# Retention block on one core: q and k of three heads by a seven-product scheme over halves of the tokens

## The chip, the cores and the metric

The kernel runs on one core of one Trainium2 chip. A core has a matrix engine (PE, with weight loads listed as PEld), a vector engine (DVE), a scalar engine (ACT), a general engine (POOL) and a queue engine (SP), which here only issues transfers. The metric is the device time of one execution in microseconds (us), as the median of several runs; lower is better.

## The reference

One encoder layer over 512 tokens of width 1024, in float32. A normalised input is multiplied by one wide matrix `w_in`, whose columns hold a short gated convolution, the queries and keys of four heads (256 columns each per head), values and gates (512 each per head) and two branch gates. What matters here is the part of q and k:

```python
h = rmsnorm(x, g_mix[l])
proj = h @ w_in[l]
...
qf = rotary(q.reshape(b, s, RET_HEADS, RET_QK_DIM)) * (RET_QK_DIM ** -0.5)
kf = rotary(k.reshape(b, s, RET_HEADS, RET_QK_DIM))

def rotary(t):            # cos, sin: position times frequency
    t1, t2 = t[..., : d // 2], t[..., d // 2:]
    return jnp.concatenate([t1 * cos - t2 * sin, t1 * sin + t2 * cos], axis=-1)
```

Behind it stand the retention itself (scores, decay, product with v, norm and gate), the merge with the convolution branch, an output projection, a gated feed-forward part and a last norm.

## The kernel before

All large products are made in three matmuls: both operands are split into a high part (rounded to the format fp32r) and a low rest, and high times high, high times low and low times high are summed in PSUM. The split of a weight tile of 128 x 1024 is a cast on ACT (line 167, tile `whi`) and a subtraction on DVE (line 168, tile `wlo`); there are five pairs of these tiles.

The weights come in the order of one list, `PLAN` (lines 56 to 116). An entry "c" is a block of 128 x 2048 numbers, used as it is; an entry "q" is one of seven forms (`FORMS`, line 51) of a matrix cut into two by two blocks: b11, t1, t2, b21, t3, t4, b22. The forms t1 to t4 are sums of blocks, which DVE makes in place in the raw tile (line 240) before the split. With them a product of 2 x 2 blocks takes seven products of blocks instead of eight; the sums on the side of the activations are made once (`sums`, line 594). `take` hands out the next weights and keeps at least two units made ahead (`AHEAD`).

The input stage runs head by head (line 636): for the heads behind the first a quad of the forms gives v and gate (`do_quad`, `strassen`, token-major, matmuls of 512 columns, line 365), and `do_qk` gives q and k. `do_qk` calls `feature_major` twice, for q and for k: a block of weights with 256 columns, two PSUM banks of 128 features x 512 tokens, 24 matmuls of 512 tokens into each (lines 280 to 282). The rotation takes the first bank as t1 and the second as t2 and is made by DVE in operations of 128 x 512: two products and one sum or difference for each half of the features (lines 616 to 618). The result is split into `hi` and `lo` (`keep`, line 556) and POOL stores both in DRAM.

`fm_quad` (line 324) is the form that the convolution's projections use later: seven products of 24 matmuls over 256 tokens (`prod`, line 321), with the result of a product being two feature blocks side by side in a bank, and combinations of the banks by ACT copies (`snap`, line 372) and DVE.

Small tiles of 128 x 512 (`t512`) come from one pool of nine, PSUM has eight banks. A scheduler sets the order of the instructions on each engine from the written program and its dependencies; so the splits and sums of later weights stand between the rotations of earlier ones, and the decay tables (`decays`, line 524, written behind the quads) are made in the first two v and gate quads. An engine carries out its own instructions in that order.

Of the kernel before, what the change touches and what calls it, by code (L numbers as in the profile page):

```python
# [12 lines left out]
F32 = mybir.dt.float32  # L13
F32R = mybir.dt.float32r
AF = mybir.ActivationFunctionType
ALU = mybir.AluOpType

P = 128
# [5 lines left out]
QK = 256  # L24
# [5 lines left out]
C_XC, C_GB, C_GC, C_Q, C_K, C_V, C_G, C_GA, C_GR = (  # L30
    0, 1024, 2048, 3072, 4096, 5120, 7168, 9216, 10240)
# [19 lines left out]
FORMS = ("b11", "t1", "t2", "b21", "t3", "t4", "b22")  # L51
# [4 lines left out]
def plan():  # L56

    out = []

    def a(name, col):
        out.append(("c", name, 0, 8, col, 256))

    def b(name, row, nk, col, nc):
        out.append(("c", name, row, nk, col, nc))

    def quad(c0, c1):
        for name in FORMS:
            for u in (0, 2):
                out.append(("q", ("w", c0, c1), name, u, 2))

    for c in (C_V, C_G):
        for r in (0, 512):
            b("w_in", r, 4, c, 512)
    for h in range(HEADS):
        if h:  # L80
            quad(C_V + h * VD, C_G + h * VD)
        a("w_in", C_Q + h * QK)
        a("w_in", C_K + h * QK)
    for c in (0, 512):
        quad(C_GA + c, C_GR + c)
    for c0, c1 in ((C_XC, C_GC), (C_XC + 256, C_GC + 256), (C_GB, C_GB + 256)):
        for name in FORMS:
            out.append(("q", ("x", c0, c1), name, 0, 4))
    for s in (2, 3):
        for c in (C_XC, C_GC, C_GB):  # L90
            a("w_in", c + s * 256)
    for h in range(HEADS):
        for c in (0, 512):
            b("w_r_out", h * VD, 4, c, 512)
    for name in FORMS:
        for u in (0, 2):
            out.append(("q", ("a",), name, u, 2))
    for r in (0, 512):
        for c in (0, 512):
            b("w_o", r, 4, c, 512)  # L100
    def f(q, *names):
        for n in names:
            out.append(("q", ("f", q), n, 0, 4))

    f(0, "b11", "b21", "b12", "b22")
    f(1, "b11", "b21")
    for q0, n in FF_PARTS:
        for q in range(max(q0, 1), q0 + n):
            f(q, *(x for x in FORMS[1:5] if q > 1 or x != "b21"))
            if q + 1 < NQ:  # L110
                f(q + 1, "b11")
            f(q, "t4", "b22")
        for name in FORMS:
            for u in range(0, n, 2):
                out.append(("q", ("d", q0), name, u, min(2, n - u)))
    return out


PLAN = plan()
BLOCKS = [x for x in PLAN if x[0] == "c"]  # L120

# [17 lines left out]
def block_kernel(ctx: ExitStack, tc: tile.TileContext, xT, xtok, wpack, wquad, cols, decs, rot, g_ffn, g_final, out):  # L139
    nc = tc.nc  # L140
# [11 lines left out]
    def misctile(n, name):  # L152
        return misc.tile([P, D + 8], F32, tag="misc", name=name)[:, 0:n]
# [4 lines left out]
    def t512(dt=F32):  # L158
        return tmp.tile([P, 512], dt, tag="t512", name="t512")

    def bank():
        return psum.tile([P, 512], F32, tag="bank", name="bank")

    def split(src, hi, lo, scale=None):

        if scale is None:
            nc.scalar.copy(hi, src)  # L167
            nc.vector.tensor_tensor(out=lo, in0=src, in1=hi.bitcast(F32), op=ALU.subtract)  # L168
        else:
            nc.scalar.activation(hi, src, AF.Copy, scale=scale)  # L170
            nc.vector.scalar_tensor_tensor(
                out=lo, in0=src, scalar=scale, in1=hi.bitcast(F32),
                op0=ALU.mult, op1=ALU.subtract)
# [85 lines left out]
    def take():  # L259
        if not ready:  # L260
            prefetch()
        x, units = ready.pop(0)
        while sum(len(u) for _, u in ready) < AHEAD and prefetch():
            pass
        return x, units
# [22 lines left out]
    def feature_major(rhs, evict, block0=0):  # L288

        c = Chunk()  # L290
        for m in range(2):
            ps = bank()
            for k in range(8):
                mm3(ps, c.w(k, m * P, P), act_pair(rhs, k), k == 0, k == 7)
            evict(block0 + m, ps)
# [17 lines left out]
    def prod(w, x, ps, start, stop=True):  # L313

        (wh, wl), (xh, xl) = w, x
        for s in range(2):
            o = ps[:, s * 256:(s + 1) * 256]
            for k in range(4):
                c = slice(k * 256 + s * P, k * 256 + (s + 1) * P)
                for i, (l, r) in enumerate(((wh, xh), (wh, xl), (wl, xh))):  # L320
                    nc.tensor.matmul(o, l[:, c], r[:, k], start=start and s == 0 and k == 0 and i == 0,  # L321
                                     stop=stop and k == 3 and i == 2, skip_group_check=True)

    def fm_quad(forms, ev11, ev21, ev22, ev12):

        def w():
            return take()[1][0]
        a, d, b = bank(), bank(), bank()
        prod(w(), forms["a11"], a, True)
        p1 = snap(a)  # L330
        prod(w(), forms["s1"], d, True)
        prod(w(), forms["s2"], a, False)
        u2 = snap(a)
        prod(w(), forms["a12"], b, True)
        nc.vector.tensor_tensor(out=p1, in0=b, in1=p1, op=ALU.add)
        ev11(p1)
        prod(w(), forms["s3"], a, False)
        u3 = snap(a)
        nc.vector.tensor_tensor(out=u3, in0=d, in1=u3, op=ALU.subtract)
        ev22(u3)  # L340
        prod(w(), forms["a22"], a, False)
        ev21(a)
        prod(w(), forms["s4"], d, False)
        nc.vector.tensor_tensor(out=u2, in0=d, in1=u2, op=ALU.subtract)
        ev12(u2)
# [24 lines left out]
    def snap(ps):  # L370
        t = t512()
        nc.scalar.copy(t, ps)  # L372
        return t
# [27 lines left out]
    def of(pair, o=0):  # L401
        return lambda k, sl: tuple(t[:, k, sl.start + o:sl.stop + o] for t in pair)
# [36 lines left out]
    rcs = misctile(D, "rcs").rearrange("p (i n) -> p i n", i=2)  # L439
# [102 lines left out]
    def kept(name):  # L542
        return dram.tile([P, 4, 512], F32, name=name)

    tabs = [dram.tile([P, 896], F32, name=f"tab{h}") for h in range(HEADS)]
    qkd = [(kept(f"qh{h}"), kept(f"ql{h}")) for h in range(HEADS)]
# [9 lines left out]
    def keep(dst, src):  # L556
        hi, lo = t512(F32R), t512(F32R)
        split(src, hi, lo)
        for d, t in zip(dst, (hi, lo)):
            store(d, t.bitcast(F32))  # L560

    def store(dst, t):
        nc.gpsimd.dma_start(dst, t)
# [6 lines left out]
    for dst, func in ((vd[0], AF.Copy), (sgd[0], AF.Silu)):  # L570
        def ev(nb, ps):
            t = t512()
            nc.scalar.activation(t, ps, func, scale=rtok[0][:, nb:nb + 1])
            store(dst[:, nb, :], t)
# [19 lines left out]
    def sums(a11, a12, a21, a22):  # L594
        out = {}
        for name, o, in0, in1, op in (
                ("s1", a22, a21, a22, ALU.subtract), ("s3", a21, a11, a21, ALU.subtract),
                ("s2", a11, a22, a11, ALU.subtract), ("s4", a12, a12, a11, ALU.add)):
            nc.vector.tensor_tensor(out=o, in0=in0, in1=in1, op=op)
            out[name] = form_tile()  # L600
            split(o, *out[name])
        return out

    xf = sums(*(xs[i][:, :, o:o + 256] for o in (0, 256) for i in range(2)))
    for n, i, o in (("a11", 0, 0), ("a12", 1, 0), ("a22", 1, 256)):
        xf[n] = tuple(t[i][:, :, o:o + 256] for t in xg)
    xforms = {n: of(t) for n, t in xf.items()}

    def do_qk(h):
        for j in range(2):  # L610
            pss = []
            feature_major(xg, lambda m, ps: pss.append(ps))
            cos, sin = rcs[:, 0, :], rcs[:, 1, :]
            for i, (c1, c2, op) in enumerate(((cos, sin, ALU.subtract), (sin, cos, ALU.add))):
                a, b = t512(), t512()
                nc.vector.tensor_tensor(out=a, in0=pss[0], in1=c1, op=ALU.mult)
                nc.vector.tensor_tensor(out=b, in0=pss[1], in1=c2, op=ALU.mult)
                nc.vector.tensor_tensor(out=a, in0=a, in1=b, op=op)
                keep([t[:, 2 * j + i, :] for t in qkd[h]], a)
# [16 lines left out]
    for h in range(HEADS):  # L636
        if h:
            do_quad(vd[h], sgd[h], AF.Silu)
        do_qk(h)
    for j in range(2):  # L640
        do_quad(gad[j], grd[j], AF.Sigmoid, AF.Sigmoid)
    decays()
# [50 lines left out]
    T1, T2 = slice(0, 256), slice(256, 512)  # L693
# [104 lines left out]
    p = do_scores(nxt[0], nxt[1])  # L798
# [3 lines left out]
    for h in range(HEADS):  # L802
# [3 lines left out]
        t = sg  # L806
        if h < HEADS - 1:
            p = do_scores(nxt[0], nxt[1])
# [15 lines left out]
    for names, hl in zip((("a11", "a12"), ("s1", "s3"), ("s2", "s4"), ("a22",)), zd):  # L824
        t = [big.tile([P, 2, 4, 256], F32R, tag="big", name="zform") for _ in hl]
# [279 lines left out]
    a, d, b = ([bank(), bank()] for _ in range(3))  # L1105
# [93 lines left out]
```

## Time and profile before

| What | us |
|---|---|
| median of 3 runs (range) | 1051.09 (1050.66 to 1052.85) |
| the profiled execution | 1050.25 |
| its span, first to last instruction | 1048.5 |
| PE busy | 1030.8 |
| DVE busy | 877.8 |
| ACT busy | 520.2 |
| one v and gate quad, 168 matmuls of 512 columns | 38.08 |
| one q and k block, 96 matmuls of 512 tokens | 21.76 |
| one `fm_quad` of the convolution, 168 matmuls of 256 tokens | 20.38 and 20.40 |

Busy times overlap, since the engines run beside each other. The chain of the page goes back from the last instruction to what released it at each step; it tells which engine's work sets the end. The first q and k block lies from 55.5 to 77.4 us, the others at 115.48, 175.32 and 235.16 us, each behind the v and gate quad of its head.

### The profile page before, as it was taken

The page shows a single profiled execution, that of the slowest core. Times are in us where ns is not written, and L with a number is a line of the kernel's source. Part 1 is how long each engine was busy: PE and PEld are TensorE (multiplying, and loading weights), DVE is VectorE, ACT ScalarE, POOL GpSimd, SP SyncE. Part 2 cuts the span into 40 slices and gives each one's busy share as a digit, 9 for nine tenths or more (in the row PEclk, how much of TensorE's full clock was granted, in tenths as well). Part 3 has the DMA queues.
Part 4 walks back from the last instruction along what each step waited for, and adds up shares of the span by engine and source line. Part 5 has one row for each costly group of instructions (what it writes and reads, how often), then busy time and mean ns, then how long its engine had stood idle before and what let it go on. Part 6 is the DMA issues. An engine that isn't in the chain of part 4 may idle for free.

```text
span 1048.5 us, 14888 instructions
## 1 busy us (share of the span) xinstructions
PE 1030.8 (98%) x5664; PEld 897.9 (86%) x5664; DVE 877.8 (84%) x1131; ACT 520.2 (50%) x697; POOL 126.3 (12%) x202
## 2 busy tenths in 40 slices
PE   8999999999999999999999989999999999999996
PEld 7788888888888998888878868889998999899985
DVE  6999786958777888698988987659998999889995
ACT  7546654453656445242532424445555565556553
POOL 0111111111101003202122320000002000110010
PEclk9999999999999999999999999999999999999999
DMA  9636647282645577819647897731319422663322
GB/s 323 233 107 213 218 159 244 91 272 89 217 135 192 183 256 245 315 32 355 239 134 188 198 341 266 241 107 36 91 36 274 124 83 79 187 155 101 121 38 84
DMA packets 52920, 183.46 MB, mean 175 GB/s; under 512 B 6896, under 2 KB 6896, under 8 KB 49264
## 3 DMA queue, kind: packets, MB, share of 16 engines
q1 hardware_dynamic: 36592, 131.12, 36.9%
q0 software_dynamic: 16256, 51.39, 16.4%
q8 instruction: 44, 0.72, 0.3%
q14 instruction: 28, 0.23, 0.1%
HBM read 137.66 MB, written 44.83 MB: 174 GB/s over the span
## 4 chain that ended last, share of the span: by engine, by line
PE 87%; DVE 4%; DMA 3%; issue 2%; ACT 2%; POOL 1%; SPq 0%; POOLq 0%; ACTq 0%; DVEq 0%
PE bank L365 31%; PE bank L321 27%; PE bank L280 10%; PE bank L282 9%; PE bank L281 9%; DMA yr<-t 2%; DMA zform<-z 1%; DMA big<-xT 1%; DVE t L769 1%; DVE wlo L168 1%; DVE bnst L764 0%; ACT whi L167 0%; POOL bnmv L767 0%; DVE big L1099 0%; DVE big L771 0%
## 5 line engine op out<-in xcount | busy, mean ns | idle before, releaser
L167 ACT CAST whi<-raw 128x1024 fp32r<-128x1024 f32 (+1 forms) x281 | 289.0, 1032 | 288.1 <-PE bank L365 74.0
L168 DVE TENSOR_TENSOR wlo<-raw,whi 128x1024 fp32r<-128x1024 f32 (+1 forms) x281 | 335.7, 1202 | 108.5 <-ACT whi L167 107.5
L321 PE MATMUL bank<-xform,whi 128*128 128x256 f32 x1440 | 260.3, 283 | 0.0
L321 PEld LDWEIGHTS bank<-xform,whi 128*128 128x128 f32 x1440 | 224.8, 192 | 0.7 <-ACT t L372 0.6
L321 PE MATMUL bank<-xform,wlo 128*128 128x256 f32 x720 | 203.7, 283 | 0.0
L365 PE MATMUL bank<-whi,big 128*128 128x512 f32 x548 | 172.7, 390 | 0.4 <-DVE big L1117 0.4
L240 DVE TENSOR_TENSOR raw<-raw 128x1024 f32<-128x1024 f32 (+1 forms) x124 | 148.4, 1205 | 1.7 <-DMA raw<-wquad 0.4
L321 PEld LDWEIGHTS bank<-xform,wlo 128*128 128x128 f32 x720 | 138.2, 192 | 0.0
L365 PEld LDWEIGHTS bank<-whi,big 128*128 128x128 f32 x548 | 102.7, 188 | 23.3 <-issue 0.8
L365 PE MATMUL bank<-wlo,big 128*128 128x512 f32 x274 | 106.7, 390 | 0.0
L365 PE MATMUL bank<-whi,xform 128*128 128x512 f32 x320 | 101.0, 389 | 0.0
L280 PE MATMUL bank<-whi,big 128*128 128x512 f32 x240 | 94.6, 396 | 2.6 <-ACT big L170 2.0
L281 PE MATMUL bank<-wlo,big 128*128 128x512 f32 x240 | 94.2, 393 | 0.0
L282 PE MATMUL bank<-whi,big 128*128 128x512 f32 x240 | 93.5, 393 | 0.1
L372 ACT COPY t<-bank 128x512 f32<-128x512 f32 x120 | 68.6, 586 | 37.8 <-PE bank L365 17.2
L280 PE MATMUL bank<-big,whi 128*128 128x512 f32 x224 | 87.1, 389 | 0.0
L281 PE MATMUL bank<-big,whi 128*128 128x512 f32 x224 | 87.1, 389 | 0.0
L282 PE MATMUL bank<-big,wlo 128*128 128x512 f32 x224 | 87.1, 389 | 0.0
L365 PEld LDWEIGHTS bank<-whi,xform 128*128 128x128 f32 x320 | 60.1, 188 | 12.5
L167 ACT CAST big<-t 128x512 fp32r<-128x512 f32 (+1 forms) x60 | 34.7, 580 | 61.8 <-DVE t L743 43.1
L365 PE MATMUL bank<-wlo,xform 128*128 128x512 f32 x160 | 62.2, 389 | 0.0
L365 PEld LDWEIGHTS bank<-wlo,big 128*128 128x128 f32 x274 | 51.4, 188 | 10.4
(175 smaller groups left out, 1416.2 us busy)
## 6 DMA issues: line engine op xcount, KB each, us to landing
raw<-wquad SPq DMA_DIRECT2D x124, 512.0 KB, 4.4
raw<-wpack SPq DMA_DIRECT2D x58, 512.0 KB, 5.2
z<-t POOLq DMA_DIRECT2D x24, 256.0 KB, 5.4
yr<-t POOLq DMA_DIRECT2D x24, 256.0 KB, 7.8
zform<-z POOLq DMA_DIRECT2D x6, 1024.0 KB, 13.0
v<-t POOLq DMA_DIRECT2D x16, 256.0 KB, 4.8
sg<-t POOLq DMA_DIRECT2D x16, 256.0 KB, 3.2
qh<-t POOLq DMA_DIRECT2D x16, 256.0 KB, 2.6
```

The source lines that it names most:

```text
L167: nc.scalar.copy(hi, src)
L168: nc.vector.tensor_tensor(out=lo, in0=src, in1=hi.bitcast(F32), op=ALU.subtract)
L240: nc.vector.tensor_tensor(out=t, in0=t, in1=raws[quad, more, u][:, 0:n], op=ALU.add)
L280: nc.tensor.matmul(ps, lh, rh, start=first, stop=False)
L281: nc.tensor.matmul(ps, lh, rl, start=False, stop=False)
L282: nc.tensor.matmul(ps, ll, rh, start=False, stop=last)
L321: nc.tensor.matmul(o, l[:, c], r[:, k], start=start and s == 0 and k == 0 and i == 0, stop=stop and k == 3 and i == 2, skip_group_check=True)
L365: nc.tensor.matmul(pss[tt], l, r[:, c], start=start and k == 0 and i == 0, stop=stop and k == n - 1 and i == 2, skip_group_check=True)
L372: nc.scalar.copy(t, ps)
L769: nc.vector.tensor_scalar(out=t, in0=ps, scalar1=mv[:, 0:1], scalar2=mv[:, 3:4], op0=ALU.subtract, op1=ALU.mult)
```

## The change

For the second to fourth head, q and k are one 2 x 2 problem: the two blocks of columns are q and k of the head (256 features each), and the tokens are cut into halves of 256. `fm_quad` makes it in seven products. Each of its four results is one of q or k for one half of the tokens, with the two halves of its features side by side in a tile of 128 x 512; the rotation multiplies both at once by the cosine and by the sine, each read twice, then makes a difference and a sum of 128 x 256. The split and the stores follow per result, with pieces of 256 tokens. The first head stays as it was.

```diff
@@ plan
     for h in range(HEADS):
         if h:
             quad(C_V + h * VD, C_G + h * VD)
-        a("w_in", C_Q + h * QK)
-        a("w_in", C_K + h * QK)
+            for name in FORMS:
+                out.append(("q", ("x", C_Q + h * QK, C_K + h * QK), name, 0, 4))
+        else:
+            a("w_in", C_Q)
+            a("w_in", C_K)
...
+    def qk_quad(h):
+
+        def ev(j, t):
+            def turned(ps):
+                ps = ps.rearrange("p (m t) -> p m t", m=2)
+                a, b = (t512().rearrange("p (m t) -> p m t", m=2) for _ in range(2))
+                for o, i in ((a, 0), (b, 1)):
+                    nc.vector.tensor_tensor(out=o, in0=ps, in1=rcs[:, i:i + 1, t].broadcast_to([P, 2, 256]),
+                                            op=ALU.mult)
+                nc.vector.tensor_tensor(out=a[:, 0], in0=a[:, 0], in1=b[:, 1], op=ALU.subtract)
+                nc.vector.tensor_tensor(out=a[:, 1], in0=a[:, 1], in1=b[:, 0], op=ALU.add)
+                hl = [t512(F32R).rearrange("p (m t) -> p m t", m=2) for _ in range(2)]
+                split(a, *hl)
+                for d, x in zip(qkd[h], hl):
+                    store(d[:, 2 * j:2 * j + 2, t], x.bitcast(F32))
+            return turned
+        T1, T2 = slice(0, 256), slice(256, 512)
+        fm_quad(xf, ev(0, T1), ev(0, T2), ev(1, T2), ev(1, T1))
...
     for h in range(HEADS):
         if h:
             do_quad(vd[h], sgd[h], AF.Silu)
-        do_qk(h)
+            qk_quad(h)
+        else:
+            do_qk(h)
```

Lines of the changed kernel are three higher from `fm_quad` on (168 becomes 171, 240 becomes 243, 321 becomes 324) and 22 to 24 higher behind `do_qk`. The order on the engines changes with it. The places below are those at which PE and DVE, or PE and ACT, meet.

On DVE in the third head (the second of the changed ones), before: the rotation of q with the weight sums (`raw`) and splits (`wlo`) of the next quad between its steps.

```order
L616 TENSOR_TENSOR t512_1564<-bank_1514,rcs_142 128x512
L168 TENSOR_TENSOR wlo_1595<-raw_1432,whi_1594 128x1024
L240 TENSOR_TENSOR raw_1432<-raw_1432,raw_1500 128x1024
L617 TENSOR_TENSOR t512_1565<-bank_1539,rcs_142 128x512
L168 TENSOR_TENSOR wlo_1680<-raw_1414,whi_1679 128x1024
L618 TENSOR_TENSOR t512_1564<-t512_1564,t512_1565 128x512
L240 TENSOR_TENSOR raw_1414<-raw_1414,raw_1586 128x1024
L168 TENSOR_TENSOR t512_1570<-t512_1564,t512_1569 128x512
```

The same place in the changed kernel, from the split of the quad's first weights (`wlo_1788`) on, the first twelve of the 31 operations up to the split of its b21; L338 is the sum of `fm_quad` that gives the first result.

```order
L171 TENSOR_TENSOR wlo_1788<-raw_1633,whi_1787 128x1024
L243 TENSOR_TENSOR raw_1633<-raw_1633,raw_1696 128x1024
L338 TENSOR_TENSOR t512_1631<-bank_1601,t512_1631 128x512
L171 TENSOR_TENSOR wlo_1830<-raw_1663,whi_1829 128x1024
L619 TENSOR_TENSOR t512_1728<-t512_1631,rcs_142 128x512
L619 TENSOR_TENSOR t512_1729<-t512_1631,rcs_142 128x512
L243 TENSOR_TENSOR raw_1663<-raw_1663,raw_1740 128x1024
L621 TENSOR_TENSOR t512_1728<-t512_1728,t512_1729 128x256
L622 TENSOR_TENSOR t512_1728<-t512_1728,t512_1729 128x256
L171 TENSOR_TENSOR wlo_1880<-raw_1633,whi_1879 128x1024
L171 TENSOR_TENSOR t512_1735<-t512_1728,t512_1734 128x512
L171 TENSOR_TENSOR wlo_1899<-raw_1663,whi_1898 128x1024
```

In these 31 operations stand 7 weight splits, 4 weight sums, 14 operations of 128 x 512 and 6 of 128 x 256. The fourth head has the same order.

On ACT in the second head, before: the casts of the next quad's weights (`whi`) and of the rotated tiles (`t512` from `t512`); `whi_1296` is the quad's b21.

```order
L167 CAST t512_1197<-t512_1192 128x512
L167 CAST whi_1280<-raw_976 128x1024
L167 CAST whi_1296<-raw_1220 128x1024
L167 CAST t512_1208<-t512_1203 128x512
L167 CAST whi_1312<-raw_1239 128x1024
```

In the changed kernel the quad's b21 is `whi_1396`, and `t512_1308` is the tile of the fourth and last rotation.

```order
L170 CAST t512_1223<-t512_1217 128x512
L170 CAST whi_1363<-raw_1077 128x1024
L170 CAST t512_1265<-t512_1259 128x512
L170 CAST whi_1380<-raw_1107 128x1024
L170 CAST t512_1308<-t512_1302 128x512
L170 CAST whi_1396<-raw_1320 128x1024
L375 COPY t512_1358<-bank_1314 128x512
```

The cast of b21 stood ahead of the last rotation's cast and now stands behind it.

On PE at the same place, before: the last matmul of the quad's t1 (`whi_1242`), then t2 (`whi_1263`, `whi_1280`), then b21.

```order
L365 MATMUL bank_1217<-whi_1242,xform_573 128x512
L365 MATMUL bank_1214<-whi_1263,xform_581 128x512
L365 MATMUL bank_1215<-whi_1263,xform_581 128x512
L365 MATMUL bank_1214<-whi_1280,xform_581 128x512
L365 MATMUL bank_1218<-whi_1296,big_553 128x512
```

In the changed kernel (t1 is `whi_1342`, t2 `whi_1363` and `whi_1380`):

```order
L368 MATMUL bank_1317<-whi_1342,xform_573 128x512
L368 MATMUL bank_1318<-whi_1396,big_553 128x512
L368 MATMUL bank_1314<-whi_1363,xform_581 128x512
L368 MATMUL bank_1315<-whi_1363,xform_581 128x512
L368 MATMUL bank_1314<-whi_1380,xform_581 128x512
```

One matmul of b21 now stands ahead of the whole of t2 (rows between the shown ones, of the same tiles, are left out).

On DVE ahead of the third decay table (L536 before, L539 now), before:

```order
L391 TENSOR_TENSOR t512_950<-bank_761,t512_950 128x512
L168 TENSOR_TENSOR wlo_1007<-raw_1002,whi_1006 128x1024
L534 TENSOR_SCALAR tab_2722<-delta_2705,lgam_221 128x896
L168 TENSOR_TENSOR wlo_1011<-raw_1003,whi_1010 128x1024
L536 TENSOR_TENSOR scr_2721<-scr_2721,tab_2722 128x896
```

and in the changed kernel:

```order
L394 TENSOR_TENSOR t512_954<-bank_761,t512_954 128x512
L171 TENSOR_TENSOR wlo_1005<-raw_914,whi_1004 128x1024
L243 TENSOR_TENSOR raw_914<-raw_914,raw_933 128x1024
L243 TENSOR_TENSOR raw_933<-raw_933,raw_962 128x1024
L171 TENSOR_TENSOR wlo_1022<-raw_914,whi_1021 128x1024
L537 TENSOR_SCALAR tab_3022<-delta_3005,lgam_221 128x896
L243 TENSOR_TENSOR raw_914<-raw_914,raw_962 128x1024
L539 TENSOR_TENSOR scr_3021<-scr_3021,tab_3022 128x896
```

Three weight sums and one more split stand there now, since the forms of q and k need sums which their plain blocks didn't.

## The prediction

> **What bounds the kernel now.** I read the page first: busy times and the chain that ended last.
>
> ```profile
> span 1048.5 us, 14888 instructions
> PE 1030.8 (98%) x5664; PEld 897.9 (86%) x5664; DVE 877.8 (84%) x1131; ACT 520.2 (50%) x697; POOL 126.3 (12%) x202
> PE 87%; DVE 4%; DMA 3%; issue 2%; ACT 2%; POOL 1%; SPq 0%; POOLq 0%; ACTq 0%; DVEq 0%
> ```
>
> PE carries 87% of the chain, so a shorter PE stage shortens the kernel, as long as PE doesn't begin to wait. DVE, at 84%, is the engine nearest to making it wait. The profiled execution took 1050.25 us, 1.75 outside its span; the median of the runs is 1051.09, 0.84 above it, and I add my sum to the median.
>
> Next the stretches of the second to fourth head, and of the two product quads of the conv branch that already run in the form the change uses (start:end, length, then busy time of PE, PEld, DVE, ACT, POOL, clock, DMA share, GB/s).
>
> ```profile
> 115.48:137.24 21.76, 21.76 (x97) 18.02 (x97) 18.16 (x23) 10.65 (x13) 3.04 (x6) 1.00 0.38 140
> 175.32:197.08 21.76, 21.76 (x97) 18.02 (x97) 17.11 (x20) 6.53 (x9) 3.23 (x6) 1.00 0.30 119
> 197.08:235.16 38.08, 38.08 (x169) 31.54 (x169) 27.24 (x29) 20.96 (x26) 5.40 (x10) 1.00 0.66 223
> 235.16:256.92 21.76, 21.76 (x97) 18.02 (x97) 17.12 (x20) 6.53 (x9) 3.24 (x6) 1.00 0.28 97
> 333.12:353.50 20.38, 20.38 (x171) 20.22 (x170) 16.32 (x17) 10.06 (x12) 1.07 (x2) 1.00 0.40 129
> 353.50:373.90 20.40, 20.40 (x170) 20.24 (x170) 18.53 (x21) 10.14 (x12) 0.00 (x0) 1.00 0.82 304
> ```
>
> The three q and k blocks that change are the 21.76 us rows. PE is busy in all of each, as it is in the v and gate quads between them (38.08). So PE has no wait here that could be removed; DVE has about 4.6 us of slack in a block and 10.8 in a quad.
>
> ```profile
> 137.24 38.08 PE bank L365 x168
> 804.42 80.63 PE bank L321 x672
> ```
>
> These two pieces of the chain give PE's pace: 38.08/168 = 0.2267 us for a matmul of 512 tokens, 80.63/672 = 0.1200 for one of 256.
>
> **PE's saving.** A block loses 96 matmuls of 512 (21.76) and gets 7 products of 24 matmuls of 256. The nearest rows are the conv quads, 20.4 us for the same 168 matmuls: 1.36 a head, 4.1 in all. By the 0.1200 of the FFN it would be 20.16, so 1.60 and 4.8. I take 4.1, the same routine on the same inputs; 4.8 is the other end.
>
> **DVE's new load.** Start-to-start times on DVE, in a stretch in which it never waits, and at narrow operations:
>
> ```profile
> 130.03 0.69 DVE L618 TENSOR_TENSOR t<-t,t 128x512 f32<-128x512 f32 x1
> ...
> 142.49 0.69 DVE L616 TENSOR_TENSOR t<-bank,rcs 128x512 f32<-128x512 f32 x1
> 143.09 0.68 DVE L617 TENSOR_TENSOR t<-bank,rcs 128x512 f32<-128x512 f32 x1
> ...
> 147.16 1.22 DVE L240 TENSOR_TENSOR raw<-raw 128x1024 f32<-128x1024 f32 x1
> 148.29 1.22 DVE L168 TENSOR_TENSOR wlo<-raw,whi 128x1024 fp32r<-128x1024 f32 x1
> ...
> 394.38 0.42 DVE L673 TENSOR_TENSOR t<-t,big 128x256 f32<-128x256 f32 x1
> 394.71 1.22 DVE L168 TENSOR_TENSOR wlo<-raw,whi 128x1024 fp32r<-128x1024 f32 x1
> ```
>
> Operations follow each other after 1.135 us (1024 wide), 0.60 (512) and 0.335 (256), less than the durations 1.22, 0.69 and 0.42 beside them. The old block has 4 weight splits and 16 operations of 512: 4 x 1.135 + 16 x 0.60 = 14.1. The new one has 7 splits, 4 weight sums (L240), 3 combinations of fm_quad, and per quarter 2 products with the rotation, 2 of 256, 1 split: 11 x 1.135 + 15 x 0.60 + 8 x 0.335 = 24.2. PE needs 20.4 in that time: DVE turns into the slower engine for the block, and the work must be made ahead, into the five weight buffers, or the next quad must absorb it.
>
> [...]
>
> ```profile
> 118.03 1.03 ACT L167 CAST whi<-raw 128x1024 fp32r<-128x1024 f32 x1
> 118.97 0.63 ACT L626 ACTIVATE t<-t 128x512 f32<-128x512 f32 x1
> ...
> 130.75 0.62 ACT L167 CAST t<-t 128x512 fp32r<-128x512 f32 x1 [3.53 <-DVE t L618]
> ```
>
> ACT's cast of a weight tile lets the next instruction start after 0.94, and its result counts after 1.05; a cast of 512 takes 0.62 to its result. The last row starts 0.72 after L618 of the fence before it: 0.12 from DVE's pace to ACT's start. ACT gets 3 casts of weights and 3 copies of a bank more per head (4.6 us); it was busy 6.5 of 21.76, which hides them.
>
> **Third and fourth head: 1.6 us of wait each.** I follow the order of the changed program from the moment PE ends the third product, t2, which frees a weight buffer. ACT casts into it: 1.05, and 0.2 for the handoff from PE (an estimate from the 0.12 above), so 1.25. From that tile's split DVE has 7 splits, 4 sums, 14 operations of 512 and 6 of 256 up to the split of the next quad's b21 that PE wants: 11 x 1.135 + 14 x 0.60 + 6 x 0.335 = 22.9, and 0.1 until it counts: 24.25. PE has meanwhile four products (4 x 2.91 = 11.65), the quad's b11 and t1 (48 x 0.2267 = 10.9) and two matmuls of b21 (0.45): 23.0. That leaves 1.25 of wait. Two or three operations that use the result just before them add some 0.1 each, so 1.6, and 3.2 for two heads. If DVE begins half a microsecond earlier it is 0.7 a head; if each of some ten handoffs costs 0.1, it is 2.3. PE's queue behind that wait is the rest of b21 and t2, all of the quad; the quad's own DVE work (27.24 busy in 38.08) leaves the room to catch up.
>
> **Second head: 3.7 us.** Here the decay tables' last two rounds lie in the same stretch (DVE first, then ACT):
>
> ```profile
> 106.20 1.22 DVE L168 TENSOR_TENSOR wlo<-raw,whi 128x1024 fp32r<-128x1024 f32 x1 [0.26 <-ACT whi L167]
> ...
> 111.85 1.09 DVE L536 TENSOR_TENSOR scr<-scr,tab 128x896 f32<-128x896 f32 x1
> ...
> 119.78 0.69 DVE L534 TENSOR_SCALAR tab<-delta,lgam 128x896 f32<-128x896 f32 x1 [1.74 <-DMA tab<-tab]
> ```
>
> ```profile
> 113.00 1.28 ACT L537 ACT_TABLE_LOAD   x1 [1.39 <-issue]
> 114.30 0.96 ACT L537 ACTIVATE tab<-scr 128x896 f32<-128x896 f32 x1
> ```
>
> The fourth round (L534) waits for the store of the third table. In the new order three weight sums and a split stand between the split at 106.20 and the third L536: 106.20 + 1.14 + 2 x 1.135 + 0.1 + 1.135 + 0.6 + 1.135 = 112.6, so L536 runs 112.6 to 113.6 instead of 111.85 to 112.85. ACT then casts two weight tiles before the table load: 112.7 + 1.89 = 114.6, the load to 115.9, the exponential to 116.8 instead of 115.3. So L534 comes 1.5 later, 121.3, and its L536 ends at 123.0. From there DVE has 8 splits, 4 sums, 14 of 512 and 8 of 256 to the last addition of the fourth rotation: 13.6 + 8.4 + 2.7 = 24.7. One of its splits, wanted after three others at 126.4, has its cast behind the fourth table load, exponential and a bank copy (123.1 + 1.28 + 0.96 + 0.5 + 1.05 = 126.9): 0.4 more, 148.1. ACT casts that rotation's tile (0.65) and, behind it, the tile of the next quad's b21 (1.05): 149.8. PE has one matmul of that b21 ahead of the whole t2. It gets there at 115.48 + 20.4 + 10.9 = 146.8. Wait: 3.0, then 0.3 for the copies of the bank that t2 adds to, which stand on ACT behind that cast, and 0.4 for dependent operations: 3.7. If the table store isn't late it is 2.2; with ten handoffs of 0.1, 4.7.
>
> **Edits that cost nothing here.** The weights' transfers are four of 512 KB per head before and after, now asked for up to four steps ahead. POOL issues eight stores per head before and after, in rows of 1 KB instead of 2:
>
> ```profile
> qh<-t POOLq DMA_DIRECT2D x16, 256.0 KB, 2.6
> ...
> z<-t POOLq DMA_DIRECT2D x24, 256.0 KB, 5.4
> ```
>
> The nearest row with 1 KB pieces is z, 5.4 us to landing against 2.6. A new block takes 19 of the nine t512 buffers in 20.4 us, so one comes round after some 9.7 us; a tile's cast, issue (0.54) and 5.4 are below 7. I take nothing, with 1.4 a head as the other end (half of the 2.8 that each landing is later). The rest of the program, from the sigmoid quads on, keeps its order, and shifts by the same amount.
>
> **The sum.** -4.1 (PE) + 3.7 (second head) + 3.2 (third and fourth) = +2.8: 1051.1 + 2.8 = 1053.9 us. With the low ends of the waits (2.2 + 1.4) and 4.8 of saving it is 1049.9; with the high ends (4.7 + 4.6) 1056.3.
>
> **Rivals.** First, the other side: DVE hides its load. The place is the split of b21 in each head; if DVE has made that split before PE arrives, there is no wait, and the kernel takes 1051.1 - 4.1 = 1047.0 (1046.3 by the other pace). It decides at 1.25 to 1.6 us less of DVE's chain per head, and 3.7 in the second. For it speaks that DVE has 10.8 us of slack in the quad before; against it that only five weight tiles can be made ahead and that rotations can't be.
>
> Second, the clock falls in the second head. The trace shows what a pause does to PE:
>
> ```profile
> 613.17 0.39 PE L282 MATMUL bank<-whi,big 128*128 128x512 f32 x1
> 615.52 0.47 PE L365 MATMUL bank<-whi,zform 128*128 128x512 f32 x1 [1.97 <-DMA zform<-z]
> 615.83 0.40 PE L365 MATMUL bank<-wlo,zform 128*128 128x512 f32 x1
> 617.91 1.12 PE L365 MATMUL bank<-whi,zform 128*128 128x512 f32 x2 [1.69 <-DMA zform<-z]
> ```
>
> ```profile
> 617.90:622.00 4.10, 4.09 (x11) 3.23 (x12) 1.21 (x2) 0.00 (x0) 0.53 (x1) 0.58 1.01 420
> ```
>
> With two matmuls between 613.6 and 617.9 the granted clock of the next 4.1 us was 0.58, which loses 0.42 x 4.1 = 1.7 us. A wait of 3.7 could do the same: 1055.6. [...]
>
> Third, DVE's operations follow each other at their full duration: the 22.9 become 11 x 1.22 + 14 x 0.69 + 6 x 0.42 = 25.6, 2.7 more per head, 1053.9 + 8.1 = 1062. The rows at 142.49 and 147.16 speak against it; the products with a repeated rotation table and of two blocks at a time have no row. Fourth, the t512 buffers bind through the 1 KB stores: 1.4 a head, 1058.1.
>
> **How the numbers follow.** The forecast case 0.53, of its own 1052.0 to 1056.3; hidden 0.13; clock 0.18; full duration 0.07; buffers 0.09. The range 1050.0 to 1059.5 leaves out the hidden case and the full durations, 0.20. About 0.2% (2.1 us) is what a measurement here tells from no change: faster, below 1049.0, is the hidden case, 0.13; within are four tenths of the forecast case and a little of the clock's, 0.23; slower 0.64.
>
> **What the changed profile would show.** PE's three blocks of 168 matmuls at 20.2 to 20.4 us. One wait of PE of 3 to 4 us at about 147, released by ACT's weight cast, and one of about 1.6 in each of the next two quads (near 210 and 270), released by DVE's split. DVE without a pause for 20 us ahead of each. The granted clock 1.00 at 150. I am wrong if PE waits inside a block, if the waits are missing, or if the stages behind 333 change their length.

## The result and the profile after

The changed kernel takes 1056.18 us (median of 6 runs, 1055.15 to 1058.32) against 1050.88 for the kernel before on the same chip (6 runs, 1050.22 to 1052.85): a ratio of 1.0051, 95% interval 1.0041 to 1.0062. It is 5.3 us slower. The forecast was 2.8 us slower, 1053.9. Execution times of one kernel spread over 3 us and more, so what follows goes by stretches of the traces more than by medians.

The page of the changed kernel begins:

```profile
span 1053.4 us, 15393 instructions
PE 1029.2 (98%) x5880; PEld 904.7 (86%) x5880; DVE 906.4 (86%) x1173; ACT 532.8 (51%) x715; POOL 130.5 (12%) x202
PE 60%; DVE 6%; DMA 3%; issue 2%; ACT 1%; POOL 1%; POOLq 0%; ACTq 0%; DVEq 0%
```

PE is busy 1.6 us less in a span that is 4.9 us longer, and DVE 28.6 us more. By stretches, in the same columns as in the prediction (start:end, length, then busy time of PE, PEld, DVE, ACT and POOL, the granted clock, DMA share, GB/s): a block of q and k with the quad behind it, for the second, third and fourth head (the fourth in one row for a block with most of a quad and one for the rest, up to the conv branch).

```profile
114.96:179.22 64.26, 60.70 (x337) 52.68 (x336) 55.06 (x67) 36.72 (x45) 10.14 (x16) 0.97 0.53 178
179.22:239.57 60.35, 58.75 (x337) 51.54 (x336) 54.71 (x64) 33.25 (x42) 10.07 (x16) 1.00 0.48 175
239.57:299.62 60.05, 58.45 (x336) 51.34 (x335) 54.49 (x65) 34.16 (x43) 10.06 (x16) 1.00 0.51 176
299.62:337.97 38.35, 38.35 (x170) 31.74 (x170) 28.68 (x29) 21.97 (x29) 4.31 (x8) 1.00 0.51 165
...
114.96:129.35 14.39, 14.39 (x122) 14.39 (x120) 11.59 (x13) 12.57 (x14) 1.13 (x2) 1.00 0.64 210
134.15:140.00 5.85, 5.85 (x48) 5.85 (x49) 5.85 (x9) 1.52 (x2) 1.22 (x2) 1.00 0.26 90
```

Before, a block and a quad were 21.76 + 38.08 = 59.84. They are now 64.26 and 60.35: 4.4 and 0.5 more. The third pair with the rest is 98.40 against 97.97: 0.4 more. Together 5.3; since the first quad ended 0.35 earlier in this execution, the conv branch starts 5.0 later (338.13 against 333.12 in the chains), and the stages behind it keep their length: its first quads take 55.13 before and after. The block itself, in two parts because PE runs some matmuls of the next quad between them (the last two rows), is 20.24: PE's saving is real, 1.52 here. The loss is in waits, and the waits of PE in the three heads are these (us in total, how often, the longest):

```profile
PE bank L368 <- ACT whi L170: 3.3, 1, 3.3
PE bank L368 <- DVE wlo L171: 3.2, 2, 1.6
...
PE bank L324 <- ACT t L375: 0.3, 1, 0.3
```

The first stands in PE's timeline of the second head; the gap between the first and the second row is the wait, and from 151.4 on matmuls of 512 start 0.43 apart instead of 0.2267:

```profile
146.38 0.39 PE L368 MATMUL bank<-whi,xform 128*128 128x512 f32 x1
150.02 0.51 PE L368 MATMUL bank<-whi,big 128*128 128x512 f32 x1 [3.25 <-ACT whi L170]
...
150.84 0.39 PE L368 MATMUL bank<-wlo,xform 128*128 128x512 f32 x1
...
152.04 1.05 PE L368 MATMUL bank<-whi,xform 128*128 128x512 f32 x2
152.89 0.63 PE L368 MATMUL bank<-wlo,xform 128*128 128x512 f32 x1
...
155.17 0.39 PE L368 MATMUL bank<-wlo,xform 128*128 128x512 f32 x1
```

```profile
151.00:155.00 4.00, 4.00 (x13) 3.10 (x12) 4.00 (x4) 1.83 (x2) 0.00 (x0) 0.57 0.31 106
155.00:159.00 4.00, 4.00 (x19) 3.31 (x18) 3.88 (x6) 2.69 (x4) 0.00 (x0) 1.00 0.71 201
```

The granted clock was 0.57 in the mean of four microseconds and 1.00 from then on. From the starts: 12 matmuls between 150.84 and 155.17 took 4.33 where 12 x 0.2267 = 2.72, so the clock cost 1.6 us. Times "by starts" are those from the start of one matmul to the start of the next, less the 0.2267 that the first one takes; they are a little longer than the waits that the rows show in brackets. The second head's ledger is -1.52 (PE) + 0.57 (a wait for a bank copy at 134.15, with its restart) + 3.41 (the pause, by starts) + 0.37 (restart and bank copy behind it) + 1.61 (clock) = 4.4. The third and fourth: -1.52 + 1.76 (the wait of 1.60, by starts) + 0.2 of restarts = 0.45 each.

### The profile page after: what moved, and what is told of

It reads as the page before. It is cut to its first block, busy times and chain, and to the rows that moved or that the text cites. A ratio compares the mean times of both kernels' runs of the same rounds, so it can differ in the third digit from the quotient of the medians.

```text
span 1053.4 us, 15393 instructions
## 1 busy us (share of the span) xinstructions
PE 1029.2 (98%) x5880; PEld 904.7 (86%) x5880; DVE 906.4 (86%) x1173; ACT 532.8 (51%) x715; POOL 130.5 (12%) x202
## 4 chain that ended last, share of the span: by engine, by line
PE 60%; DVE 6%; DMA 3%; issue 2%; ACT 1%; POOL 1%; POOLq 0%; ACTq 0%; DVEq 0%
PE bank L324 23%; PE bank L368 19%; PE bank L283 6%; PE bank L285 6%; PE bank L284 6%; DVE wlo L171 2%; DMA yr<-t 2%; DMA zform<-z 1%; DVE raw L243 1%; ACT whi L170 1%; DVE t L793 1%; DVE bnst L788 0%; DMA raw<-wquad 0%; POOL bnmv L791 0%; DVE big L1123 0%
## 5 line engine op out<-in xcount | busy, mean ns | idle before, releaser
L170 ACT CAST whi<-raw 128x1024 fp32r<-128x1024 f32 (+1 forms) x290 | 297.8, 1033 | 294.4 <-DVE raw L243 62.3
L171 DVE TENSOR_TENSOR wlo<-raw,whi 128x1024 fp32r<-128x1024 f32 (+1 forms) x290 | 345.8, 1203 | 89.7 <-ACT whi L170 86.9
L324 PE MATMUL bank<-xform,whi 128*128 128x256 f32 x1632 | 295.2, 283 | 0.0
L324 PEld LDWEIGHTS bank<-xform,whi 128*128 128x128 f32 x1632 | 254.7, 192 | 0.7 <-ACT t L375 0.6
L324 PE MATMUL bank<-xform,wlo 128*128 128x256 f32 x816 | 230.9, 283 | 0.0
L243 DVE TENSOR_TENSOR raw<-raw 128x1024 f32<-128x1024 f32 x136 | 162.7, 1207 | 2.4 <-DMA raw<-wquad 1.0
L324 PEld LDWEIGHTS bank<-xform,wlo 128*128 128x128 f32 x816 | 156.6, 192 | 0.0
L368 PEld LDWEIGHTS bank<-whi,big 128*128 128x128 f32 x548 | 102.8, 188 | 27.3 <-ACT whi L170 3.7
L375 ACT COPY t<-bank 128x512 f32<-128x512 f32 x129 | 73.8, 585 | 38.9 <-PE bank L368 17.8
L283 PEld LDWEIGHTS bank<-whi,big 128*128 128x128 f32 x240 | 45.4, 189 | 14.1 <-ACT big L173 2.6
L285 PEld LDWEIGHTS bank<-whi,big 128*128 128x128 f32 x240 | 45.5, 190 | 10.2 <-DVE big L174 0.5
L324 PE MATMUL bank<-big,whi 128*128 128x256 f32 x288 | 53.2, 285 | 0.3 <-ACT t L375 0.3
```

The lines of the kernel that those rows point to most:

```text
L243: nc.vector.tensor_tensor(out=t, in0=t, in1=raws[quad, more, u][:, 0:n], op=ALU.add)
L283: nc.tensor.matmul(ps, lh, rh, start=first, stop=False)
L285: nc.tensor.matmul(ps, ll, rh, start=False, stop=last)
L368: nc.tensor.matmul(pss[tt], l, r[:, c], start=start and k == 0 and i == 0, stop=stop and k == n - 1 and i == 2, skip_group_check=True)
```

## Experiments

Theory: the new block gives DVE and ACT more work than PE's time covers, so PE waits for weight tiles in the next quad, and the longest of these waits lowers the clock. The rivals were a fixed loss per head, a clock that falls for another reason, ACT's order, and a form that saves PE nothing. Ratios are to the kernel before on the same chip, whose median there was 1051.5 us (the two kernels with some heads changed, eight matmuls, no rotations), 1051.9 (three matmuls, GpSimd, late tables, one more buffer) and 1052.0 (the last three). The ratio and its interval are those on record; the two medians alone give a ratio that differs from it by up to 0.001, about 1 us, and differences in us below are by the ratio on record.

**The second head alone, and the other two alone.**

```diff
-        if h:
-            ... seven products
+        if h == 1:     # in the other kernel: h > 1; both in plan() and in the loop
+            ... seven products
```

> Only the second head's q and k take the seven products; the third and fourth are as before. Theory (DVE and ACT are late after the second head's block, and the pause then lowers the clock): -1.4 of PE work, +3.5 of wait near 150, +1.7 for a clock near 0.5 behind it: +3.8, about 1054.8 us against 1051. Rival 1 (the clock would have fallen somewhere anyway and has nothing to do with that pause): +2.1, about 1053.1. Rival 2 (the loss is the same in each head, a third of the 5.3): +1.8, about 1052.8.

Measured: 1054.6 us, ratio 1.0039 (1.0024 to 1.0055), 4.1 us slower (3.1 by the medians). The theory had 3.8, the rivals 2.1 and 1.8, so the time alone favours the theory without much room. The trace decides: the wait is 3.26, the clock behind it 0.56, the stretch 64.27, 4.4 more than before; the next one, in its old form, is 59.84 as before.

> Only the third and fourth heads' q and k take the seven products. Theory: 2 x (-1.4 of PE work + 1.6 of wait on DVE's split of b21) = +0.5, about 1051.5 us, the clock 1.00 behind both waits. Rival (the loss is the same in each head): +3.5, about 1054.5. If there were no DVE chain to wait for, -2.7: 1048.3.

Measured: 1053.1 us, ratio 1.0019 (1.0008 to 1.0030), 2.0 us slower. An equal loss per head (3.5) lies outside the interval, 0.8 to 3.2, but so does the theory's 0.5. The windows show where some of the difference is:

```profile
136.83:175.61 38.78, 38.41 (x169) 31.46 (x168) 30.48 (x33) 20.93 (x27) 6.48 (x12) 1.00 0.55 191
175.61:235.95 60.34, 58.74 (x337) 51.53 (x336) 54.87 (x64) 33.49 (x42) 10.08 (x16) 1.00 0.49 174
```

The changed stretch is 60.34, 0.5 more, as in the changed kernel (the theory had 0.25 a head). The quad ahead of the first changed block is 38.78 instead of 38.08: PE waits 0.37 at 148.24 for ACT's bank copies, which came a little later than before. The theory had no term for the work around the changed blocks. With the fourth head the stretches make 1.7 in all, which lies within the interval. The profiled execution lost 2.4 us or more to the clock near 620, where nothing was changed: 11 matmuls of 512 take 4.86 there, from 619.87 to 624.73, where 11 x 0.2267 = 2.49 (last section).

**The pause filled with matmuls.** Eight matmuls of 128 (and, in a second kernel, three) stand ahead of the waiting one; the trace has two records for each.

```diff
         prod_tm(n, forms["s1"], d, True)
+        for _ in range(fill):      # 8 (or 3) in the third head's quad, 0 elsewhere
+            nc.tensor.matmul(b[0][:, 0:P], ones, ones, start=True, stop=True)
```

> The changed kernel with eight matmuls more (128 wide, of ones, into a bank that a later product overwrites) ahead of the place where PE waits at 150: they take about 1.9 us inside the wait of 3.3 and leave the result as it is. Theory that the pause lowers the clock: the wait is cut to about 1.4 and stays as long in sum, the clock behind it is 1.00: 1.7 us less than the changed kernel, about 1054.5. Rival (the clock falls for another reason, or the drop is no part of the time): 1056.2. If DVE is not late there, and PE simply runs the added matmuls: 1058.

Measured: 1054.5 us, ratio 1.0028 (1.0017 to 1.0040). PE's rows and the window behind the pause, with eight:

```profile
147.97 1.95 PE L386 MATMUL bank<-ones 128*128 128x128 f32 x16
151.39 0.74 PE L368 MATMUL bank<-whi,big 128*128 128x512 f32 x2 [1.48 <-ACT whi L170]
```

```profile
151.40:155.40 4.00, 4.00 (x18) 3.22 (x19) 4.00 (x4) 2.81 (x4) 0.87 (x2) 1.00 0.40 135
```

PE is held up as long as before (1.95 + 1.48), but the clock stays at 1.00: it fell behind the empty pause (0.57) and not behind this one. The stretch is 62.96 instead of 64.26, 1.3 shorter and not 1.6. Counted from the start of the block, the fourth table round begins 0.55 later in this execution than in the changed kernel, and PE's pause ends 0.55 later too; behind the pause the stretch is 1.85 shorter.

> As the kernel with eight matmuls in the pause, with three: about 0.7 us, so that a pause of 2.5 to 3 us is left. It is to show how long a pause lowers the clock. If a pause below 3 does nothing: clock 1.00 behind it, 1.7 us less than the changed kernel in that stretch. If the clock falls for pauses above 2.5 too: near 0.5 for 3 to 4 us behind it, as after the pause of 3.25.

Measured, one run: 1056.29 us; the stretch is 62.61, 1.65 shorter than in the changed kernel.

```profile
147.12 0.83 PE L386 MATMUL bank<-ones 128*128 128x128 f32 x6
150.53 0.74 PE L368 MATMUL bank<-whi,big 128*128 128x512 f32 x2 [2.58 <-ACT whi L170]
```

```profile
150.50:154.50 4.00, 3.97 (x17) 3.22 (x18) 4.00 (x4) 2.84 (x4) 0.91 (x2) 1.00 0.40 135
```

A pause of 2.6 left the clock alone here. That it would anywhere isn't shown: the last section has two shorter ones in a row, behind which the clock fell. One run says nothing of a fifth of a per cent; the reading rests on the stretch and the clock.

**DVE's rotations left out.** The kernel leaves out the rotation of q and k in the last three heads, and with it eight t512 tiles a block; the split reads the bank itself.

```diff
-                a, b = (t512()... for _ in range(2))
-                ... two products, difference, sum
                 hl = [t512(F32R)... for _ in range(2)]
-                split(a, *hl)
+                split(ps, *hl)
```

> The changed kernel without the rotation of q and k in the last three heads (the four products, sums and differences per quarter are left out; the bank is cast and split as it is): DVE has 4 x (2 x 0.60 + 2 x 0.335) = 7.5 us less in each block, 16.7 against PE's 20.4. Theory: all three waits and the drop of the clock go, PE's saving of 3 x 1.36 stays: 1051.0 - 4.1 = 1047.0. Rival (the waits come from ACT's casts or from the number of weight buffers, not from DVE's load): the wait near 150 stays, 1050 to 1053. Rival (the form of seven products saves PE nothing): 1051.

Measured: 1047.2 us, ratio 0.9965 (0.9953 to 0.9977). PE has no wait and the clock no drop in the three heads:

```profile
115.50:173.99 58.49, 58.49 (x337) 51.61 (x336) 48.14 (x50) 33.68 (x42) 10.10 (x16) 1.00 0.52 180
```

The next stretch, to 232.48, is 58.49 too. 58.49 against 59.84 is 1.35 less a head, the saving that the prediction took. With five weight buffers, DVE's rotations are what turns the saving into a loss.

**The same work moved to GpSimd.**

```diff
-                nc.vector.tensor_tensor(out=a[:, 0], ... op=ALU.subtract)
-                nc.vector.tensor_tensor(out=a[:, 1], ... op=ALU.add)
+                nc.gpsimd.tensor_tensor(out=a[:, 0], ... op=ALU.subtract)
+                nc.gpsimd.tensor_tensor(out=a[:, 1], ... op=ALU.add)
```

> The changed kernel with the difference and the sum of each rotated quarter (two operations 256 wide, eight per head) on GpSimd instead of DVE: DVE's chain is 8 x 0.335 = 2.7 us shorter per head. Theory: the waits of 1.6 behind the third and fourth head go; behind the second ACT's cast of b21 still stands behind the last rotation's, so that wait goes from 3.25 to about 2.4 if GpSimd takes 0.8 for each, and the clock stays at 1.00: 1051 - 4.1 + 2.4 + 0.6 for the bank copies = 1050. Rival (GpSimd takes 2 us or more for each, or slows DVE): the wait of the second head stays at 3 or more and the clock falls, 1053 or more.

Measured: 1073.8 us, ratio 1.0207 (1.0188 to 1.0225), far from the theory's 1050. The rival had said 1053 or more, if GpSimd takes 2 us or more or slows DVE. DVE's and GpSimd's rows in the third head, then PE's wait in the fourth head's quad and the window behind it:

```profile
217.65 0.68 DVE L347 TENSOR_TENSOR t<-bank,t 128x512 f32<-128x512 f32 x1
217.89 0.73 POOL L621 TENSOR_TENSOR t<-t,t 128x256 f32<-128x256 f32 x1
218.25 1.46 DVE L171 TENSOR_TENSOR wlo<-raw,whi 128x1024 fp32r<-128x1024 f32 x1
218.59 1.71 POOL L622 TENSOR_TENSOR t<-t,t 128x256 f32<-128x256 f32 x1
```

```profile
220.50 0.39 PE L368 MATMUL bank<-whi,big 128*128 128x512 f32 x1
224.08 0.60 PE L368 MATMUL bank<-wlo,big 128*128 128x512 f32 x1 [3.18 <-DVE wlo L171]
```

```profile
224.00:228.00 4.00, 3.69 (x9) 2.43 (x10) 2.72 (x4) 1.59 (x3) 2.90 (x3) 0.57 0.06 19
```

Five of the 24 operations take 0.73 or 0.74, 0.7 from start to start: 2.1 times DVE's 0.335. Beside them DVE stands still or reads a bank, as at 217.89. The other 19 take 1.57 to 2.78, and beside each of them DVE works on tiles of 128 x 1024; some of these DVE operations take 1.46 to 1.77 instead of 1.22. So the two took longer beside each other, and the rival's second condition came true.

ACT's casts of the rotated tiles come behind these sums (it waits 47.1 us in all for them between 115 and 300), DVE's splits behind the casts, and the weight tiles behind both. The waits of 1.6 became 3.2, behind each the clock now falls (0.57 from 224 to 228, 0.62 from 289.7 to 293.5), and the three stretches are 17.6 us longer than in the changed kernel.

**The decay tables made later.**

```diff
+            if left is gad[0] and tt == 0:     # after the first sigmoid quad
+                nc.vector.scalar_tensor_tensor(out=late, in0=t[:, 0:8], scalar=0.0, in1=lgam, ...)
-            ... scalar2=lgam[:, 4 + h:5 + h] ...
+            ... scalar2=late[:, 4 + h:5 + h] ...
```

> The changed kernel with the decay tables made in the second quad of the sigmoid gates (they are given an input that is ready only after the first of these quads), so that they no longer stand in the stretch of the second head. Theory: the second head then behaves as the third and fourth: -1.36 of PE work, +1.6 of wait and 0.25 of restarts, no drop of the clock: 3 x 0.5 = +1.5, 1052.5 us. Rival (the wait of 3.25 comes from the order of ACT's casts, not from the tables): 1055 to 1056. If the tables are in the way where they are now, a wait behind 300: 1054 or more, with the second head's gain seen at 180.

Measured: 1054.2 us, ratio 1.0024 (1.0014 to 1.0034), 2.5 slower than before.

```profile
115.24:175.55 60.31, 58.71 (x338) 51.53 (x336) 53.87 (x63) 31.92 (x40) 10.12 (x16) 1.00 0.49 175
175.55:235.86 60.31, 58.71 (x338) 51.53 (x337) 53.86 (x63) 31.91 (x40) 10.10 (x16) 1.00 0.50 175
```

```profile
323.80 0.95 ACT L541 ACTIVATE tab<-scr 128x896 f32<-128x896 f32 x1
324.66 1.05 ACT L375 COPY t<-bank 128x512 f32<-128x512 f32 x2
```

The second head now equals the third, 0.5 more than before and no clock drop: the tables in this stretch were what made its wait long. With them gone ACT's order is another too: the cast of b21's weights ends by 145.0, ahead of the last rotation's cast (149.37), while in the changed kernel it stands behind that. What the tables' own time and what this order does isn't separated. The tables are in the way in the new place as well: the exponential stands ahead of two bank copies on ACT, and PE waits 1.8 for those at 325.

**One more weight buffer.**

```diff
-    wpool = ctx.enter_context(tc.tile_pool(name="wpool", bufs=5))
+    wpool = ctx.enter_context(tc.tile_pool(name="wpool", bufs=6))
-    rawp = ctx.enter_context(tc.tile_pool(name="raw", bufs=10))
+    rawp = ctx.enter_context(tc.tile_pool(name="raw", bufs=8))
```

> The changed kernel with six pairs of weight buffers instead of five (and eight raw buffers instead of ten, to make room). Theory: DVE and ACT are fast enough over a quad and a block together (about 52 us of DVE work in 58.5) and are only kept from working ahead by the buffers; one tile more is 2.9 us of PE ahead: the waits of 1.6 go, the one of 3.25 goes down to 0.4 or less, the clock stays at 1.00: 1047 to 1048. Rival 1 (DVE's load in the block itself decides, buffers don't): 1055 to 1056. Rival 2 (eight raw buffers make weight transfers late in the other stages): slower than 1051, with waits on raw tiles behind 340.

Measured: 1046.0 us, ratio 0.9942 (0.9928 to 0.9956): faster than both kernels.

```profile
115.27:173.85 58.58, 58.57 (x337) 51.62 (x336) 56.87 (x69) 37.88 (x46) 10.11 (x16) 1.00 0.54 191
```

The next stretch, to 232.21, is 58.36. DVE has all its work in these stretches and PE no wait to speak of. So DVE is not too slow for a block and a quad together; with five buffers the tiles came too late. With six, ACT's order changes along with the room: PE begins b21 at 146.35, and the last weight cast before that ends at 142.8, ahead of the last rotation's cast (147.67). Which of the two does it isn't separated. Is the buffer a gain of its own? The same two numbers in the kernel before:

> The kernel before, unchanged but for six pairs of weight buffers and eight raw buffers. Theory (the sixth buffer is worth only what the change's own waits cost, and the change's saving on PE is real): no wait stands in the second to fourth head before, so nothing is to be had there; 1051, within 1 us. Rival (the sixth buffer is worth several microseconds in this kernel whatever the form of q and k): 1047 to 1049, and the change itself then saves less than 4.1 even with six buffers.

Measured: 1054.5 us, ratio 1.0025 (1.0012 to 1.0037): slower by 2.6, a miss of both guesses. PE's two new waits, in quads that are as before, and ACT ahead of each:

```profile
107.77 0.50 PE L365 MATMUL bank<-whi,big 128*128 128x512 f32 x1 [1.59 <-ACT t L372]
...
151.62 0.50 PE L365 MATMUL bank<-whi,xform 128*128 128x512 f32 x1 [1.17 <-ACT t L372]
```

```profile
106.29 0.95 ACT L537 ACTIVATE tab<-scr 128x896 f32<-128x896 f32 x1 [2.21 <-DVE scr L536]
107.15 0.57 ACT L372 COPY t<-bank 128x512 f32<-128x512 f32 x1
...
150.46 0.62 ACT L167 CAST t<-t 128x512 fp32r<-128x512 f32 x1 [1.88 <-DVE t L618]
150.99 1.07 ACT L372 COPY t<-bank 128x512 f32<-128x512 f32 x2
```

DVE comes to the table's sum and to the rotation's last sum later. Ahead of the first it waits 2.01 at 104.39 for the store of a table; the second starts at 149.71 instead of 144.82, in another order of its operations than before. ACT waits 2.21 and 1.88 for these, and the bank copies that PE wants stand behind them on ACT.

> The changed kernel with six and eight buffers once more, on the same chip as the kernel before with six and eight: theory 1046 to 1047, 4.1 us below that kernel. Rival: the difference of the two is 2 us or less.

Measured: 1046.3 us, ratio 0.9954 (0.9938 to 0.9970), on one chip with the kernel above, which is 8.2 slower: neither the theory's 4.1 nor the rival's 2. The two waits above, which the changed kernel doesn't have, are 3.1 by starts, so 4.1 and 3.1 make 7.2. In the profiled executions the clock near 620 differs as well (last section). What of the rest is due to what was not taken apart.

> The same, with three weight tiles asked for ahead in the written order instead of two. Theory: with no wait left on a weight tile in the three heads there is nothing more to gain there: 1046, within 1 us. Rival (the weights come late in other stages too): 1044 or less. If casts and splits asked for earlier now stand ahead of bank copies and rotations: 1048 or more.

Here `AHEAD` is 3 instead of 2. Measured: 1045.3 us, ratio 0.9938 (0.9923 to 0.9953): within the theory's 1046 give or take 1, and the interval overlaps with that of six buffers alone. It is the fastest median of the study.

## Where the prediction held, and where it failed

**PE's saving** was taken as 1.36 a head. It is 1.35 by the stretches without DVE's rotations, and 1.52 by the second head's block in the changed kernel. Right.

**The third and fourth head** were to wait 1.6 for DVE's split of b21, near 210 and 270. They wait 1.60, at 212.65 and 272.99. The wait counts 1.76 by starts and some 0.2 follows in restarts, so 3.9 for the two instead of 3.2.

**The second head's wait** was to be 3.0, from 146.8 to 149.8. It is 3.25, from 146.77 to 150.02, released by ACT's cast of that tile, as the prediction's walk along the rows had it. DVE's and ACT's rows:

```profile
119.72 0.69 DVE L537 TENSOR_SCALAR tab<-delta,lgam 128x896 f32<-128x896 f32 x1 [1.07 <-DMA tab<-tab]
...
126.64 1.23 DVE L171 TENSOR_TENSOR wlo<-raw,whi 128x1024 fp32r<-128x1024 f32 x1 [1.70 <-PE bank L324]
...
147.61 0.43 DVE L622 TENSOR_TENSOR t<-t,t 128x256 f32<-128x256 f32 x1
```

```profile
119.97 2.94 ACT L170 CAST whi<-raw 128x1024 fp32r<-128x1024 f32 x3
122.93 1.28 ACT L540 ACT_TABLE_LOAD   x1
124.23 0.96 ACT L540 ACTIVATE tab<-scr 128x896 f32<-128x896 f32 x1
...
125.55 2.05 ACT L170 CAST whi<-raw 128x1024 fp32r<-128x1024 f32 x2
...
147.46 1.04 ACT L170 CAST whi<-raw 128x1024 fp32r<-128x1024 f32 x1 [3.51 <-DVE raw L243]
148.41 0.61 ACT L170 CAST t<-t 128x512 fp32r<-128x512 f32 x1
148.93 1.04 ACT L170 CAST whi<-raw 128x1024 fp32r<-128x1024 f32 x1
```

The fourth table began at 119.72, not 121.3. That changed nothing: ACT came to the table load at 122.93 from three weight casts (123.1 in the walk), and the cast behind the load, the exponential and a bank copy ended at 126.60 (126.9 in the walk). DVE's split starts at 126.64, right behind that cast; it waited 1.70 for it, for which the walk had 0.4, since DVE was there earlier. The row puts this wait down to PE, but PE's matmuls run on there and the same wait of 1.70 is put down to ACT's cast in the kernel with eight matmuls. From 126.64 on DVE has no pause, as was said, and ends its last rotation at 148.04 (148.1 predicted). The 0.2 between 149.8 and 150.02 is a cast that the walk left out: at 147.46 ACT casts a weight tile that waited for DVE's sum, and only behind it, at 148.41, the rotated tile. With two small waits at 134.15 and 150.5 the head's waits come to 4.35 against the 3.7 of the sum. The one at 134.15, 0.30 long, lies inside the block, which the prediction had named as a sign of being wrong.

**The clock** is the step that failed. The forecast case left it at 1.00; it was 0.57 over the four microseconds from 151, which cost 1.6 us, and that was the second rival: it had 1.7 and 1055.6, and a chance of 0.18. That 1056.2 still lies within the forecast case's own 1052.0 to 1056.3 is luck: the time came by the rival's way. With the waits' excess of 1.4 this is the difference between +2.8 and the ledger's +5.3, less 0.5 that PE saved more. The working had the trace's own row (two pauses with two matmuls between them, clock 0.58 behind them) and still gave the fall only 0.18; that a pause would seldom lower the clock was the author's estimate, and no run shows how often one does. In the changed kernel's trace the 3.41 us ahead of the drop at 151.43 hold 1.41 us of PE work (last section).

**The other rivals.** That DVE hides its load is what happens with six buffers, not with five, as the argument against it said. DVE's operations kept their distances of 1.13, 0.60 and 0.335, so the full durations are out. The stores in rows of 1 KB land as before, the median of the 16 `qh` stores, 12 of them in the new form, after 2.6 us. And with six weight buffers, where a block takes as many t512 tiles, PE has no wait to speak of in the heads, so the t512 buffers don't bind.

## What to carry to other kernels

A product form that saves matmuls pays in weight sums, splits and evictions on other engines: count these engines' time over the stretch that the weight buffers let them work ahead, not over the block alone. If the stretch is the bound, a buffer is the cheaper remedy than moving work, but try it beside the change, since alone it cost time here. Where PE waits, look at the clock too: the pause of 3.25 cost 1.6 us of clock on top here, one of 2.58 cost none; filling the first with eight small matmuls, which left 1.48 of it, went without a drop.

## What was not expected of the hardware

The length of a pause doesn't decide alone whether the clock falls. Behind the one of 2.58 with three matmuls ahead of it the clock stayed at 1.00; behind two of 1.81 and 1.70 with two matmuls between them, near 620 in the changed kernel's trace, it fell to 0.50. After the first 20 us of that trace it falls to 0.50 at 151.43, 622.47 and 1049.14, the first two for 3.41 us each. The distances, 471.04 and 426.67, are 138 and 125 times 3.413. In the GpSimd kernel the drops in the three heads begin at 139.00, 156.06, 224.33 and 289.18, which are 5, 20 and 19 times 3.413 apart. So in these two traces the drops lie whole multiples of 3.413 apart; why isn't shown. With a trace divided into stretches of that length from one of its drops, the clock behind a stretch goes with PE's busy time in it (second column of times):

```profile
148.02:151.43 3.41, 1.41 (x5) 0.98 (x6) 3.41 (x5) 3.41 (x6) 1.43 (x2) 1.00 0.21 73
151.43:154.84 3.41, 3.41 (x10) 2.64 (x9) 3.41 (x4) 1.40 (x2) 0.00 (x0) 0.50 0.23 81
154.84:158.26 3.42, 3.42 (x16) 2.81 (x16) 3.42 (x4) 1.95 (x3) 0.00 (x0) 1.00 0.67 175
```

| Kernel | stretch | PE busy in it | clock of the next stretch |
|---|---|---|---|
| changed, second head | 148.02 to 151.43 | 1.41 | 0.50 |
| changed, third head | 209.46 to 212.87 | 1.81 | 1.00 |
| changed, fourth head | 270.90 to 274.31 | 1.81 | 1.00 |
| changed, conv branch's last product | 619.06 to 622.47 | 0.70 | 0.50 |
| before, conv branch's last product | 614.63 to 618.05 | 0.84 | 0.50 |
| GpSimd, second head | 135.58 to 139.00 | 1.44 | 0.50 |
| GpSimd, third head | 220.92 to 224.33 | 0.25 | 0.50 |
| six buffers | 610.65 to 614.06 | 1.67 | 0.50 |

In the traces before and after, between 20 and 1030 us, PE is busy 1.41 us or less in the stretches ahead of a drop and 1.81 or more in all others; with six buffers it is 1.67 ahead of one. Why the pause of 2.58 went without a drop isn't shown.

At the conv branch's last product the kernel before waits 1.97 and 1.69 us and the changed one 1.81 and 1.70, with two matmuls between, and the clock falls to 0.50 for 3.41 us behind them. In the profiled executions of the last two heads alone (2.14 and 2.05) and of the kernel before with six buffers (1.85 and 1.69) matmuls of 512 start 0.43 to 0.51 apart behind the waits, for 4.9 us at least and for 5.3. In the second execution with six buffers and in the one with `AHEAD` at 3 the first of the two waits is gone, the other is about 1.85 by starts, and behind it the matmuls start 0.23 to 0.28 apart. So with nothing changed there, this product lost nothing to the clock, 1.7, or 2.4 us and more in these executions.
